# Where the normalized stream, the gated activations and the mixers' outputs begin in SBUF, relative to the weights' tiles

## The chip, the cores and the metric

The kernel runs on one core of a Trainium2 chip. The metric is the device time of one execution in microseconds (us); before the change its median over three runs is 674.23 us (674.15 to 675.28).

## The reference

A decoder trunk of two layers over a stream of 256 positions by 1024 channels, all in float32. Each layer: an RMS norm, one input projection to 2964 columns, four groups of sequence mixers (sparse attention, differential attention, an mLSTM, dilated attention) of 256 columns each, an output projection back into the stream, a second norm and a SwiGLU block of 2816 channels. A last norm follows.

```
for layer in range(DEPTH):
    h = rmsnorm(x, norm_mix[layer])
    z = h @ w_in[layer]                       # 256x1024 @ 1024x2964
    ... four mixers on z's columns ...
    x = x + concat(o_a, o_b, o_c, o_d) @ w_out[layer]          # 1024x1024
    h = rmsnorm(x, norm_ffn[layer])
    x = x + (silu(h @ w_gate[layer]) * (h @ w_up[layer])) @ w_down[layer]
return rmsnorm(x, norm_final)
```

## The kernel before

**Split products.** Every weight arrives by DMA as float32 in a tile of 128x1024 (`wraw`) and is split: ScalarE rounds it to `whi` (float32r, line 232), VectorE subtracts to get `wlo` (line 233). There are four buffers of each, 4096 bytes per partition apiece. The other side of a product is split in the same way: the normalized stream is `hT` (a high and a low part), the SwiGLU activations are `gT`, the mixers' outputs are `oT`. A product is high x high + high x low + low x high, accumulated in PSUM. A matmul holds one operand in the array, 128 columns of it (the stationary one, loaded by a weight load that the profile shows as PEld), and streams the other through (the moving one).

**Two roles.** The projections use the tiles in two ways:

- The stream's side is stationary and the weights move. This is the input projection (`zp`, function `columns`, lines 237 to 239: three matmuls of 512 columns, or 404 in one chunk), and the last down projection of the second layer (`dn` and `dnl`, function `wide`, also lines 237 to 239: three matmuls of 512 columns for three of its five accumulators, and three of 256 for the other two, `dnl`).
- The weights are stationary and the stream's side moves. This is the output projection (`op`, function `wide_T`, from `oT`), the gate and up projections (`f`, function `columns_T`, from `hT`) and the down projection of the first layer (`dn`, function `wide_T`, from `gT`). Where an accumulator has a whole PSUM bank, high and low part of the stream move as one piece of 512 columns under `whi` (line 246), and the high part alone as 256 columns under `wlo` (line 247): a pair. Where two accumulators share a bank, there are three matmuls of 256 columns (lines 237 to 239): a triple.

**Counts.** Over both layers `f` has 576 pairs and 128 triples, `op` 128 triples. The `dn` of the first layer has 132 pairs and 44 triples. The `dn` of the second layer has 198 matmuls of 512 columns and 132 of 256. `zp` has 480 matmuls of 512 columns and 96 of 404.

**Order.** The mixers are cut into steps that a table (`ORDER`) puts between the units of the input projection. The framework's scheduler then fixes one order per engine when the program is built, and moves the first matmuls of `op` in between the last steps of the mixers. Weights are fetched from SyncE's queue, each as soon as its `wraw` buffer is free.

**Places.** The pools take SBUF one after the other: constants, the small parameters (`par`), the weights (`wp`), the working tiles (`work`, where `hT` comes second and `oT` later), the small statistics and the large tile `big` that holds z, and later `gT`. Each tile's start is rounded up to 32 bytes. Before the change the built program has, per partition and in bytes:

| tile | starts at | role of its operand | its start minus the weights' start, modulo 128 |
|---|---|---|---|
| `whi`, `wlo` | 64352 and 80736, then every 4096 | | |
| `hT` (two tiles of 8192) | 99168, 107360 | stationary in `zp`, moving in `f` | 0 |
| `gT` | 180608 | moving in the first `dn`, stationary in the second | 32 |
| `oT` | 152896, then every 2048 | moving in `op` | 96 |

Blocks of `hT`, `gT` and `oT` lie 1024 bytes apart and the slices of a weight tile 512 bytes, so the last column holds for every matmul of a stage (the second half of the chunk of 404 columns excepted).

Of the kernel before, what the change touches and what calls it, by code (L numbers as in the profile page):

```python
# [10 lines left out]
F32 = mybir.dt.float32  # L11
F32R = mybir.dt.float32r
# [6 lines left out]
P = 128  # L19
SEQ = 256  # L20
D = 1024
NH = 4
HD = 64
KB = D // P
D_IN = 2964
D_FF = 2816
NFB = D_FF // P
DEPTH = 2
EPS = 1e-6
WARM = 11  # L30
MID0 = 2
TAIL = 2
MID1 = 2
# [69 lines left out]
def trunk(ctx, tc, xt, w_in, w_out, w_gu, w_dn, gains, gfin, cmpw, chan, rowp, ident_d, kf, kb, out):  # L103
# [4 lines left out]
    par = ctx.enter_context(tc.tile_pool(name="par", bufs=1))  # L108
    wp = ctx.enter_context(tc.tile_pool(name="wp", bufs=2))
    work = ctx.enter_context(tc.tile_pool(name="work", bufs=1))  # L110
# [3 lines left out]
    def mmbank(name):  # L114
        return ps.tile([P, 512], F32, name=name, tag="mm", bufs=4)

    def aux(name):
        return ps.tile([P, 512], F32, name=name, tag="aux", bufs=3)
# [4 lines left out]
    def acc4(name, n=4):  # L123
        return [(mmbank if i < 4 else aux)(f"{name}{i}") for i in range(n)]
# [7 lines left out]
    gain = const.tile([P, DEPTH, 2, KB], F32, name="gain")  # L132
# [9 lines left out]
    bigp = ctx.enter_context(tc.tile_pool(name="bigp", bufs=1))  # L142
# [23 lines left out]
    wb = aux("warm")  # L166
    for _ in range(WARM):
        T.matmul(wb, wz[:, 0:P], wz, start=True, stop=True)
# [18 lines left out]
    def bcast(ap):  # L187
        return ap.partition_broadcast(P)
# [35 lines left out]
    def weight_unit(src, parts=1):  # L224
        n = src.shape[-1]
        raw = wp.tile([P, 1024], F32, name="wraw", bufs=4)
        hi = wp.tile([P, 1024], F32R, name="whi", bufs=4)
        lo = wp.tile([P, 1024], F32R, name="wlo", bufs=4)
        for i in range(parts):
            c = slice(i * n // parts, (i + 1) * n // parts)  # L230
            nc.sync.dma_start(raw[:, c], src[:, c])
            S.activation(hi[:, c], raw[:, c], AF.Copy)  # L232
            V.tensor_tensor(out=lo[:, c], in0=raw[:, c], in1=hi[:, c].bitcast(F32), op=OP.subtract)  # L233
        return hi, lo
# [6 lines left out]
    def product_T(acc, wh, wl, x2, first, last):  # L241


        xh, xl = x2 if isinstance(x2, tuple) else (x2[:, 0], x2[:, 1])
        if acc.shape[-1] == 2 * SEQ:
            T.matmul(acc, wh, x2.rearrange("p a t -> p (a t)"), start=first, stop=False)  # L246
            T.matmul(acc[:, 0:SEQ], wl, xh, start=False, stop=last)  # L247
        else:
            product(acc, wh, wl, xh, xl, first, last)

    def rstd_of(ms, shape, name, eps=None):
# [12 lines left out]
        G.tensor_tensor(out=r, in0=e, in1=nh, op=OP.pow)  # L264
        return r


    class Norm:
        def __init__(self, g):
            self.g = g  # L270

            hl = [work.tile([P, 4, 2, SEQ], F32R, name="hT", bufs=2) for _ in range(2)]
            self.x2 = [hl[k // 4][:, k % 4] for k in range(KB)]
            self.xT = [(x[:, 0], x[:, 1]) for x in self.x2]

        def blocks(self, p):
# [59 lines left out]
    def heads(ap, n):  # L336
        return ap.rearrange("p (n w) -> p n w", n=n)
# [12 lines left out]
    def mixer_a(l, z, d):  # L350
# [25 lines left out]
        for u in range(2):  # L376
            wh, wl = cur['cmpw'][u]
            for i in range(4):
                p, cs = 4 * u + i, slice(i * 256, (i + 1) * 256)
# [34 lines left out]
                T.matmul(pcs[:, (t * 2 + b) * 30:(t * 2 + b + 1) * 30], q0[:, b, t * P:(t + 1) * P],  # L414
                         kcb.rearrange("p a n -> p (a n)"), start=True, stop=True)
        yield
        gs = work.tile([P, 2, 12], F32, name="gs")
        S.activation(gs, z[:, :, COL['ag']:COL['ag'] + 12], AF.Tanh, scale=0.5)
        V.tensor_scalar(gs, gs, 0.5, 0.5, op0=OP.mult, op1=OP.add)

# [418 lines left out]
    d = None  # L839
    for l in range(DEPTH):  # L840
        if l == 0:
            nrm = Norm(gain[:, 0, 0])
        cur['big'] = bigp.tile([P, 2 * D_IN + NS * 1024], F32, name="zbig", tag="big")
        z = cur['big'][:, 0:2 * D_IN].rearrange("p (t c) -> p t c", t=2)
        oT = [None] * 4
# [41 lines left out]
        def columns(src, w, accs, xT, ahead=None, mid=None, steps=()):  # L887

            units = []
            for u in range(KB // 2):  # L890
                if ahead:
                    ahead(u)
                units.append(weight_unit(src[:, u * 2 * w:(u + 1) * 2 * w], 2 if ahead is first_x and u == 0 else 1))
            for u in range(KB // 2):
                wh, wl = units[u]
                for t in range(2):
                    for k in range(2):
                        kk = 2 * u + k
                        xh, xl = (a[:, t * P:(t + 1) * P] for a in xT[kk])
                        cs = slice(k * w, (k + 1) * w)  # L900
                        product(accs[t], xh, xl, wh[:, cs], wl[:, cs], kk == 0, kk == KB - 1)
                if mid and u == mid[0]:
                    mid[1]()
                if u < len(steps) - 1:
                    emit(steps[u])

        def parts_of(pairs):


            return [(b[0][:, j * SEQ:(j + 1) * SEQ], j == 0, j == 1) if len(b) == 1 else (b[j], True, True)  # L910
                    for b in pairs for j in range(2)]
# [16 lines left out]
        def wide_T(src, x2, nblk, name, norm, full=False):  # L928

            if full:
                banks = [[f(f"{name}{i}{j}") for j, f in enumerate(p)]
                         for i, p in enumerate(((mmbank, mmbank), (aux, pvbank), (mmbank, mmbank), (aux,)))]
            else:
                banks = [[b] for b in acc4(name)]

            accs = parts_of(banks)

            def step(kk, m, w):  # L940
                cs = slice(m * P, (m + 1) * P)
                acc, first, last = accs[m]
                product_T(acc, w[0][:, cs], w[1][:, cs], x2(kk), kk == 0 and first, kk == nblk - 1 and last)

            tail = nblk - TAIL
            for kk in range(tail):
                w = weight_unit(src[:, kk * D:(kk + 1) * D])
                for m in range(KB):
                    step(kk, m, w)
                yield  # L950
            ws = [weight_unit(src[:, kk * D:(kk + 1) * D]) for kk in range(tail, nblk)]
            nrm = norm()

            for p in range(KB // 2):
                for m in (2 * p, 2 * p + 1):
                    for kk in range(tail, nblk):
                        step(kk, m, ws[kk - tail])
                if len(banks[p]) == 1:
                    xx = xr[:, 2 * p:2 * p + 2]
                    V.tensor_tensor(out=xx, in0=heads(banks[p][0], 2), in1=xx, op=OP.add)  # L960
                else:
                    for b, m in zip(banks[p], (2 * p, 2 * p + 1)):
                        for i in range(2):
                            V.tensor_tensor(out=xr[:, m], in0=b[:, i * SEQ:(i + 1) * SEQ], in1=xr[:, m], op=OP.add)
                nrm.blocks(p)
                nrm.squares(p)
            return nrm

        def run(g):

            while True:
                try:
                    next(g)
                except StopIteration as r:
                    return r.value
# [34 lines left out]
        for c, (c0, w) in enumerate(CHUNKS):  # L1010
            zacc.append([mmbank(f"zp{t}")[:, 0:w] for t in range(2)])
            columns(w_in[l, :, 8 * c0:8 * (c0 + w)], w, zacc[c], nrm.xT,
                    None if l else {0: first_x, 1: rest_x, 2: rest_par}.get(c),
                    (MID0, first_z) if l == 0 and c == 1 else (MID1, nrm.factors) if c == 0 and l else None,
                    ORDER[l][c].split('|'))
            if c == 1:
                cur['cmpw'] = [weight_unit(cmpw[l, :, u * 1024:(u + 1) * 1024]) for u in range(2)]
            if l or c:
                to_z(c)
            if c == len(CHUNKS) - 1:  # L1020
                fs['o'] = lambda: wide_T(w_out[l], lambda kk: tuple(a[:, kk % 2] for a in oT[kk // 2]), KB, "op",
                                         lambda: Norm(gain[:, l, 1]))
            emit(ORDER[l][c].split('|')[-1])

        def wide(src, opair, nblk, name, rows):
# [24 lines left out]
        nrm = run(gens['o'] if 'o' in gens else fs['o']())  # L1050


        if l + 1 < DEPTH:
            d = load_positions(l + 1)
            load_params(l + 1, d)
        else:
            gf = work.tile([P, D], F32, name="gfin", tag="hT", bufs=2)
            nc.sync.dma_start(gf, bcast(gfin[0]))
        gT = bigp.tile([P, NFB * 2 * SEQ], F32R, name="gT", tag="big").rearrange("p (k a t) -> p k a t", a=2, k=NFB)

        def taken(b, out=None):

# [80 lines left out]
            blk += nk  # L1143
        gp = lambda kk: gT[:, kk]
        if l + 1 < DEPTH:
            nrm = run(wide_T(w_dn[l], gp, NFB, "dn", lambda: Norm(gain[:, l + 1, 0]), True))
        else:
            wide(w_dn[l], gp, NFB, "dn", nrm.rs)

    for t in range(2):  # L1150
# [3 lines left out]
        for h in range(2):  # L1154
            hs = slice(h * 512, (h + 1) * 512)
            sq = work.tile([P, 2, SEQ], F32, name="sq", bufs=2).rearrange("p a b -> p (a b)")
            n = 2 if t and h else 1
# [130 lines left out]
```

## Time and profile before

| | us |
|---|---|
| median of three runs | 674.23 |
| the profiled execution | 673.65 |
| its span from first to last instruction | 671.7 |
| TensorE busy | 657.1 |
| VectorE busy | 481.1 |
| ScalarE busy | 384.6 |

The times below are those of the one profiled execution, which took 673.65 us: 671.7 us of span and 1.95 us around it. The duration that the trace gives a matmul is no price, since matmuls overlap. What a matmul costs is the distance from its start to the start of the next, where nothing is waited for, and that is how the rows of the timeline are read here.

The stages, by the starts of their matmuls in the timeline: the first input projection and the mixers, with the first matmuls of `op` among the mixers' last, to 135 us, the rest of `op` to 149, `f` to 275, `dn` to 336, and in the second layer projection and mixers to 460, the rest of `op` to 476, `f` to 603, `dn` to 665, and then the last norm.

### The profile page before, as it was taken

To read this page: it belongs to the slowest core of one execution; us is meant where nothing else is said; L and a number is where in the kernel's file an instruction comes from. 1 tells how busy PE (TensorE), PEld (TensorE's weight loads), DVE (VectorE), ACT (ScalarE), POOL (GpSimd) and SP (SyncE) were. 2 spreads that over 40 slices of the span, in tenths; PEclk is the share of its full clock that TensorE was granted. 3 is DMA by queue.
4 is the path that set the end of the run, shared out by engine and by line. 5 is a ranking of instruction groups with operands and counts; after the bars stand their busy time and mean duration, and the time that the engine had idled before them with its cause. 6 is when DMAs were issued, how large, how long until landed. Compare 5 with 4: busy or idle time off the path is not lost.

```text
span 671.7 us, 10554 instructions
## 1 busy us (share of the span) xinstructions
PE 657.1 (98%) x3993; PEld 567.1 (84%) x3993; DVE 481.1 (72%) x811; ACT 384.6 (57%) x689; POOL 51.1 (8%) x67
## 2 busy tenths in 40 slices
PE   8899999999999999999999999999999999999996
PEld 5787778899988888899979778779998888888885
DVE  6689698667777877744587969875867777775443
ACT  7466685555555656533466587754655656564332
POOL 0000031100200110000010001140000000000002
PEclk9999999999999999999999999999999999999999
DMA  7865414246566656666647541243556666676631
GB/s 267 295 192 157 143 30 128 64 126 192 175 198 183 190 165 207 188 191 190 181 128 235 160 123 33 63 157 95 158 187 178 190 179 190 185 211 192 188 121 62
DMA packets 31874, 109.09 MB, mean 162 GB/s; under 512 B 3920, under 2 KB 4560, under 8 KB 31824
## 3 DMA queue, kind: packets, MB, share of 16 engines
q1 hardware_dynamic: 31392, 107.89, 53.0%
q8 instruction: 31, 0.51, 0.3%
q10 hardware_dynamic: 432, 0.54, 0.2%
q14 instruction: 19, 0.16, 0.1%
HBM read 107.37 MB, written 1.05 MB: 161 GB/s over the span
## 4 chain that ended last, share of the span: by engine, by line
PE 92%; DVE 3%; ACT 2%; POOL 1%; issue 1%; DMA 1%; POOLq 0%; DVEq 0%; ACTq 0%
PE f L246 20%; PE f L247 10%; PE zp L238 6%; PE zp L239 6%; PE zp L237 5%; PE dn L246 4%; PE dn L238 3%; PE dn L237 3%; PE dn L239 3%; PE dn L247 2%; PE f L237 2%; PE f L239 2%; PE f L238 2%; PE op L239 2%; PE op L237 2%; PE op L238 2%
## 5 line engine op out<-in xcount | busy, mean ns | idle before, releaser
L233 DVE TENSOR_TENSOR wlo<-wraw,whi 128x1024 fp32r<-128x1024 f32 (+2 forms) x201 | 242.0, 1207 | 116.8 <-ACT whi L232 116.0
L232 ACT ACTIVATE whi<-wraw 128x1024 fp32r<-128x1024 f32 (+2 forms) x201 | 210.1, 1047 | 179.2 <-PE f L246 46.0
L246 PE MATMUL f<-hT,whi 128*128 128x512 f32 x576 | 203.6, 399 | 0.0
L247 PE MATMUL f<-hT,wlo 128*128 128x256 f32 x576 | 161.8, 281 | 0.0
L246 PEld LDWEIGHTS f<-hT,whi 128*128 128x128 f32 x576 | 108.2, 188 | 27.0
L247 PEld LDWEIGHTS f<-hT,wlo 128*128 128x128 f32 x576 | 108.8, 189 | 0.0
L238 PE MATMUL zp<-wlo,hT 128*128 128x512 f32 (+1 forms) x192 | 75.7, 395 | 1.3 <-DVE wlo L233 1.3
L237 PE MATMUL zp<-whi,hT 128*128 128x512 f32 (+1 forms) x192 | 74.1, 393 | 1.8 <-ACT whi L232 1.8
L239 PE MATMUL zp<-whi,hT 128*128 128x512 f32 (+1 forms) x192 | 74.9, 391 | 0.0
L246 PE MATMUL dn<-gT,whi 128*128 128x512 f32 x132 | 46.7, 390 | 0.0
L237 PEld LDWEIGHTS zp<-whi,hT 128*128 128x128 f32 x192 | 36.0, 188 | 8.3 <-ACT whi L232 3.1
L238 PEld LDWEIGHTS zp<-wlo,hT 128*128 128x128 f32 x192 | 36.3, 189 | 7.8 <-DVE wlo L233 2.7
L239 PEld LDWEIGHTS zp<-whi,hT 128*128 128x128 f32 x192 | 36.2, 188 | 5.1
L247 PE MATMUL dn<-gT,wlo 128*128 128x256 f32 x132 | 37.2, 282 | 0.0
L237 PE MATMUL f<-hT,whi 128*128 128x256 f32 x128 | 36.9, 288 | 0.0
L237 PE MATMUL op<-oT,whi 128*128 128x256 f32 x128 | 36.8, 288 | 0.0
L239 PE MATMUL op<-oT,wlo 128*128 128x256 f32 x128 | 36.6, 286 | 0.0
L238 PE MATMUL op<-oT,whi 128*128 128x256 f32 x128 | 36.5, 285 | 0.0
L239 PE MATMUL f<-hT,wlo 128*128 128x256 f32 x128 | 36.2, 283 | 0.0
L238 PE MATMUL f<-hT,whi 128*128 128x256 f32 x128 | 36.2, 283 | 0.0
L246 PEld LDWEIGHTS dn<-gT,whi 128*128 128x128 f32 x132 | 24.8, 188 | 4.4
L238 PE MATMUL dn<-wlo,gT 128*128 128x512 f32 x66 | 26.2, 397 | 0.0
(299 smaller groups left out, 1161.1 us busy)
## 6 DMA issues: line engine op xcount, KB each, us to landing
wraw<-in_w_gu_dram SPq DMA_DIRECT2D x88, 512.0 KB, 4.4
wraw<-in_w_dn_dram SPq DMA_DIRECT2D x44, 512.0 KB, 3.7
wraw<-in_w_in_dram SPq DMA_DIRECT2D x39, 512.0 KB, 4.3
wraw<-in_w_out_dram SPq DMA_DIRECT2D x16, 512.0 KB, 3.5
wraw<-in_w_in_dram SPq DMA_DIRECT2D x8, 404.0 KB, 3.2
wraw<-in_cmpw_dram SPq DMA_DIRECT2D x4, 512.0 KB, 4.7
xr<-in_xt_dram SPq DMA_DIRECT2D x4, 256.0 KB, 5.3
chan<-in_chan_dram SPq DMA_DIRECT2D x2, 261.0 KB, 4.7
```

Of the source, the lines that this page charges most:

```text
L232: S.activation(hi[:, c], raw[:, c], AF.Copy)
L233: V.tensor_tensor(out=lo[:, c], in0=raw[:, c], in1=hi[:, c].bitcast(F32), op=OP.subtract)
L237: T.matmul(acc, xh, wh, start=first, stop=False)
L238: T.matmul(acc, xh, wl, start=False, stop=False)
L239: T.matmul(acc, xl, wh, start=False, stop=last)
L246: T.matmul(acc, wh, x2.rearrange("p a t -> p (a t)"), start=first, stop=False)
L247: T.matmul(acc[:, 0:SEQ], wl, xh, start=False, stop=last)
```

## The change

No instruction is added to a compute engine, removed or put in another place on one. What changes is where tiles begin:

- `hT` is one tile of 16416 bytes instead of two of 8192, from a pool slot with one buffer instead of two. Its operand begins at the tile's start where it is stationary (`zp`) and 8 elements, 32 bytes, behind it where it moves (`f`).
- `gT` has 32 bytes more, and begins 32 bytes behind its tile's start in the first layer (moving), at its start in the second (stationary).
- The small tile `gs` goes from the working pool to the parameters' pool, which lies ahead of the weights, and a tile of 32 bytes (`pad`), which nothing uses, stands behind `hT`.

```
-            hl = [work.tile([P, 4, 2, SEQ], F32R, name="hT", bufs=2) for _ in range(2)]
-            self.x2 = [hl[k // 4][:, k % 4] for k in range(KB)]
+            hl = shifted(work.tile([P, KB * 2 * SEQ + SHIFT], F32R, name="hT", bufs=1), KB, moving)
+            self.x2 = [hl[:, k] for k in range(KB)]
...
+    def shifted(a, n, moving):
+        a = a[:, SHIFT if moving else 0:]
+        return a[:, 0:n * 2 * SEQ].rearrange("p (k a t) -> p k a t", a=2, k=n)
...
-        gs = work.tile([P, 2, 12], F32, name="gs")
+        gs = par.tile([P, 2, 12], F32, name="gs")
...
-            nrm = Norm(gain[:, 0, 0])
+            nrm = Norm(gain[:, 0, 0], False)
+
+            work.tile([P, PAD], F32, name="pad")
...
-                                         lambda: Norm(gain[:, l, 1]))
+                                         lambda: Norm(gain[:, l, 1], True))
...
-            gf = work.tile([P, D], F32, name="gfin", tag="hT", bufs=2)
+            gf = work.tile([P, D], F32, name="gfin", tag="hT", bufs=1)
...
-        gT = bigp.tile([P, NFB * 2 * SEQ], F32R, name="gT", tag="big").rearrange("p (k a t) -> p k a t", a=2, k=NFB)
+        gT = shifted(bigp.tile([P, NFB * 2 * SEQ + SHIFT], F32R, name="gT", tag="big"), NFB, l + 1 < DEPTH)
...
-            nrm = run(wide_T(w_dn[l], gp, NFB, "dn", lambda: Norm(gain[:, l + 1, 0]), True))
+            nrm = run(wide_T(w_dn[l], gp, NFB, "dn", lambda: Norm(gain[:, l + 1, 0], False), True))
```

`SHIFT` and `PAD` are 8. In the built program the weights' tiles then start at 64448 and 80832, `hT` at 99264, `gT` at 180672 and `oT` at 152960, and the differences become:

| stage | moving side | the stream's side minus the weights' start, modulo 128: before | now |
|---|---|---|---|
| `zp` | weights | 0 | 0 |
| `op` | mixers' outputs | 96 | 64 |
| `f` | stream | 0 | 32 |
| `dn`, first layer | gated activations | 32 | 32 |
| `dn`, second layer | weights | 32 | 0 |

The weights' own start modulo 64 goes from 32 to 0.

Since `hT` has one buffer now, the last norm's gain (`gfin`, which takes that slot at the very end) can be fetched only when all of `hT` has been read, and not half of it. On SyncE's queue near the end of the second layer's `f`, before the change, where `w_dn` is the down projection's weight:

```order
36 L231 DMA wraw<-in_w_dn_dram 128x1024 x5
37 L1058 DMA gfin<-in_gfin_dram 128x1024
38 L231 DMA wraw<-in_w_dn_dram 128x1024 x17
```

and with the change:

```order
36 L233 DMA wraw<-in_w_dn_dram 128x1024 x7
37 L1068 DMA gfin<-in_gfin_dram 128x1024
38 L233 DMA wraw<-in_w_dn_dram 128x1024 x15
```

The fetch of `gfin` has moved behind two weights. On the other engines the same instructions stand in the same order, with the same waits, but for the number of the DMA's semaphore near this place.

## Rows read from the trace of the kernel before

**Rows 1.** The page: busy time of TensorE and VectorE with share of the span and instructions; the granted clock in 40 slices of the span; the chain that ended last, by engine.

```profile
PE 657.1 (98%) x3993; PEld 567.1 (84%) x3993; DVE 481.1 (72%) x811; ACT 384.6 (57%) x689; POOL 51.1 (8%) x67
...
PEclk9999999999999999999999999999999999999999
...
PE 92%; DVE 3%; ACT 2%; POOL 1%; issue 1%; DMA 1%; POOLq 0%; DVEq 0%; ACTq 0%
```

**Rows 2.** Waits of TensorE over the whole span: who waited for whom, us in total, times, the longest.

```profile
PE zp L237 <- ACT whi L232: 1.8, 2, 1.1
PE cT L357 <- ACT zbig L987: 1.7, 2, 1.4
PE zp L238 <- DVE wlo L233: 1.3, 3, 0.5
```

**Rows 3.** Busy time of each engine by stage: the stretch in us and its length, then busy us (instructions) of PE, PEld, DVE, ACT and POOL, the granted clock, the DMA engines' busy share and GB/s.

```profile
143.00:160.00 17.00, 17.00 (x145) 17.00 (x144) 14.72 (x23) 11.42 (x18) 0.00 (x0) 1.00 0.52 151
...
173.00:275.00 102.00, 102.00 (x581) 88.44 (x580) 79.12 (x107) 59.16 (x89) 15.56 (x10) 1.00 0.63 186
275.00:336.00 61.00, 61.00 (x397) 55.80 (x396) 32.43 (x40) 25.81 (x30) 0.00 (x0) 1.00 0.66 193
336.00:460.00 124.00, 121.62 (x717) 100.00 (x716) 100.46 (x215) 82.17 (x188) 16.24 (x20) 1.00 0.40 122
...
501.00:603.00 102.00, 102.00 (x580) 88.44 (x579) 77.14 (x105) 59.51 (x89) 0.00 (x0) 1.00 0.64 187
603.00:665.00 62.00, 62.00 (x332) 52.78 (x330) 30.37 (x34) 25.09 (x32) 3.14 (x3) 1.00 0.50 152
```

**Rows 4.** Timeline of TensorE, starts and modelled durations in us: the first pair of `f` and the first matmul of `dn` behind the last one, in the first layer and in the second. Between the two starts lie 288 pairs each time.

```profile
173.23 0.40 PE L246 MATMUL f<-hT,whi 128*128 128x512 f32 x1
...
274.99 0.40 PE L246 MATMUL dn<-gT,whi 128*128 128x512 f32 x1
...
501.28 0.40 PE L246 MATMUL f<-hT,whi 128*128 128x512 f32 x1
...
603.05 0.40 PE L237 MATMUL dn<-whi,gT 128*128 128x512 f32 x1
```

**Rows 5.** The same view, the end of the first layer's `dn`: twelve matmuls of 256 columns, four triples, from the first of these rows to the last, which is the next layer's first.

```profile
334.76 0.28 PE L237 MATMUL dn<-gT,whi 128*128 128x256 f32 x1
334.87 0.28 PE L238 MATMUL dn<-gT,whi 128*128 128x256 f32 x1
...
336.04 0.28 PE L239 MATMUL dn<-gT,wlo 128*128 128x256 f32 x1
336.16 0.39 PE L237 MATMUL zp<-whi,hT 128*128 128x512 f32 x1
```

**Rows 6.** The same view, the last triples of `f` ahead of its first pair: the first of the seven matmuls of 256 columns that lie between it and the pair at 173.23, and the last.

```profile
172.39 0.28 PE L239 MATMUL f<-hT,wlo 128*128 128x256 f32 x1
...
173.11 0.28 PE L239 MATMUL f<-hT,wlo 128*128 128x256 f32 x1
```

**Rows 7.** The same view, two undisturbed stretches of `zp` of 512 columns, one in each layer: from the first row to the second twelve matmuls, and from the third to the fourth twelve.

```profile
34.09 0.39 PE L237 MATMUL zp<-whi,hT 128*128 128x512 f32 x1
...
36.80 0.39 PE L237 MATMUL zp<-whi,hT 128*128 128x512 f32 x1
...
365.90 0.40 PE L237 MATMUL zp<-whi,hT 128*128 128x512 f32 x1
...
368.66 0.39 PE L237 MATMUL zp<-whi,hT 128*128 128x512 f32 x1
```

**Rows 8.** The same view, the second layer's `dn`: nine matmuls of 512 columns lie between its start at 603.05 and the first row here, and six of 256 between the two rows here.

```profile
605.15 0.28 PE L237 MATMUL dnl<-whi,gT 128*128 128x256 f32 x1
...
605.87 0.40 PE L237 MATMUL dn<-whi,gT 128*128 128x512 f32 x1
```

**Rows 9.** The same view, `op`: eighteen matmuls of 256 columns from the first row to the second.

```profile
136.21 0.28 PE L237 MATMUL op<-oT,whi 128*128 128x256 f32 x1
...
138.34 0.28 PE L237 MATMUL op<-oT,whi 128*128 128x256 f32 x1
```

**Rows 10.** The instructions of line 246, which are the 512 columns of a pair: durations in ns, least, median and most, and first and last start.

```profile
L246 PE MATMUL f<-hT,whi x576: 395/398/403, 173.2 to 602.7; 128*128 128x512 f32 x192
...
L246 PE MATMUL dn<-gT,whi x132: 390/390/399, 275.0 to 334.4; 128*128 128x512 f32 x132
```

**Rows 11.** What ScalarE waited for between 180 and 260 us, in `f`: us in total, times, the longest.

```profile
ACT whi L232 <- PE f L246: 14.1, 12, 1.8
```

**Rows 12.** Timeline of SyncE's queue around the fetch of the last norm's gain; and of the view of that tile its first readers, on GpSimd (ns, first and last start in us), and the fetch's time from issue to landing.

```profile
585.68 11.98 SPq L231 DMA_DIRECT2D wraw<-in_w_dn_dram  x5
597.72 1.21 SPq L1058 DMA_DIRECT2D gfin<-in_gfin_dram  x1
599.87 11.73 SPq L231 DMA_DIRECT2D wraw<-in_w_dn_dram  x5
...
L1163 POOL TENSOR_TENSOR y<-xs,gfin x2: 1290/1296/1302, 657.9 to 663.5; 128x512 f32<-128x512 f32 x2
...
DMA to landing us min/median/max: 6.8/6.8/6.8
```

More of the change, by code (lines that the diff above doesn't have):

```diff
@@ L30 @@
 WARM = 11
+SHIFT = 8
+PAD = 8
 MID0 = 2
@@ L265, in rstd_of, with __init__ @@
         return r
+    def shifted(a, n, moving):
+        a = a[:, SHIFT if moving else 0:]
+        return a[:, 0:n * 2 * SEQ].rearrange("p (k a t) -> p k a t", a=2, k=n)
     class Norm:
-        def __init__(self, g):
+        def __init__(self, g, moving):
             self.g = g
-            hl = [work.tile([P, 4, 2, SEQ], F32R, name="hT", bufs=2) for _ in range(2)]
-            self.x2 = [hl[k // 4][:, k % 4] for k in range(KB)]
+            hl = shifted(work.tile([P, KB * 2 * SEQ + SHIFT], F32R, name="hT", bufs=1), KB, moving)
+            self.x2 = [hl[:, k] for k in range(KB)]
             self.xT = [(x[:, 0], x[:, 1]) for x in self.x2]
```

## The prediction

> **What bounds the kernel now.** I read the page first: TensorE is busy for 657.1 of 671.7 us, 92% of the chain that ended last are its instructions, and its clock is granted in full, at the upper of its two levels (2.4 GHz), in every slice and stage [rows 1, 3]. Its waits come next: the three longest lines come to 4.8 us over the whole span, all in the input projection and the mixers, none in `op`, `f` or `dn` [rows 2]. The table by stage says the same: in `f`, in `dn` and in the pure part of `op` TensorE is busy without a gap, while VectorE and ScalarE have room (79.12 and 59.16 us of 102 in `f`) [rows 3]. So in these stages time is the number of matmuls times the distance from one start to the next. The matmuls' counts, sizes, order and waits stay as they are, so the change can work only through that distance, and the question is whether the distance depends on where the two operands lie.
>
> It does differ between stages that do the same work. A pair, 512 columns under `whi` and then 256 under `wlo`, takes (274.99 - 173.23) / 288 = 353.3 ns in the first layer's `f`, and (603.05 - 501.28) / 288 = 353.4 ns in the second's [rows 4]. The first layer's `dn` is made of the same pairs and of triples. Four triples at its end take 336.16 - 334.76 = 1.40 us, 116.7 ns a matmul [rows 5]. From 274.99 [rows 4] to 336.16 [rows 5] are 61.17 us; less 132 matmuls at 116.7 ns, 15.40 us, 45.77 us are left for 132 pairs: 346.7 ns. The triples of `f` go the same way: (173.23 - 172.39) / 7 = 120.0 ns a matmul [rows 4, 6] against 116.7 in `dn`. What the two stages don't share is the distance of the moving operand from the weights, modulo 128 bytes: 0 in `f`, 32 in `dn`. The durations carry the same mark: the 512 columns show 395 to 403 ns in `f`, and 390 both at the least and at the median in `dn` [rows 10].
>
> Where the weights move, the sign is the other way. `zp` has distance 0 and takes (36.80 - 34.09) / 12 = 225.8 ns per 512 columns in one clean stretch and (368.66 - 365.90) / 12 = 230.0 in another [rows 7]. The second layer's `dn` has distance 32 and takes (605.15 - 603.05) / 9 = 233.3 [rows 4, 8]. I have no mechanism for this turn of sign, so I carry a price over only between stages in which the same side moves.
>
> **The change part by part.** Each number is a count times a difference of the distances above.
>
> - `f`, pairs: distance 0 becomes 32, which is that of the first `dn`, with the same side moving and the same order of matmuls. 576 pairs x (353.3 - 346.7) = 3.8 us off. Bounds: 0, if the place has no part in it, and 3.8, since `f` has the dearest pairs of the trace and `dn` the cheapest.
> - `f`, triples: 384 matmuls x (120.0 - 116.7) = 1.3 us off, with bounds 0 and 1.3 for the same reason.
> - The second `dn`, 512 columns: distance 32 becomes 0, that of `zp`. `zp` gives 225.8 to 230.0; I take their middle, 228, and 233.3 for the row replaced: 198 x 5.3 = 1.0 us off, bounds 0.7 (by 230.0) and 1.5 (by 225.8). Its 132 matmuls of 256 columns now take (605.87 - 605.15) / 6 = 120.0 ns [rows 8]. No row has this size at distance 0 with the weights moving; by the triples' two distances it could gain 0.4 us or, since 120.0 is already the worse of the two, nothing. I take 0.
> - `op`: distance 96 becomes 64, which no stage has. It takes (138.34 - 136.21) / 18 = 118.3 ns now [rows 9], between the 116.7 and the 120.0 of the other triples. Bounds for 384 matmuls: 0.6 us off, if 64 is like 32, 0.65 us more, if it is like 0. I take 0, in the middle of two ends that are equally near.
> - The first `dn` and `zp` keep their distances (32 and 0): 0, and a cost only if something other than the distance counts (a rival below).
> - The mixers' own matmuls see their tiles move by 64 to 160 bytes against each other. Of the 3993 matmuls [rows 1] 3222 belong to the projections, 771 don't; a tenth of these at the 3.3 ns of a triple's matmul would be 0.25 us either way. I take 0.
> - One buffer for `hT` instead of two tiles: the next norm writes into it only after `dn` has begun, long after `f` has read it, so no wait arises. The one instruction that moves is the fetch of the last gain. It was issued at 597.72, between two groups of weights, and will be issued when `f` ends, near 603, ahead of an eighth weight that can't go earlier: its `wraw` buffer is freed by a split that itself waits for `f`'s last unit. The fetch lands after 6.8 us [rows 12], and the gain is first read at 657.9. 0; if the weight behind it were held up, a delay of one issue, 1.2 us [rows 12], is covered by the three split units ahead.
>
> Does the gain reach the end? In `f` TensorE is followed by everybody: ScalarE's split waited 14.1 us for it within 80 us [rows 11], so weights, at 186 GB/s and 0.63 of the DMA engines' time, are ahead [rows 3]. With pairs 1.9% shorter VectorE's load goes from 78% to 79%. Nothing else comes due.
>
> The sum for the profiled execution: 3.8 + 1.3 + 1.0 = 6.1 us off 673.65, which is 671.7 of span and 1.95 around it: 667.55. The profiled execution lies 0.58 us below the median of the runs shown, so the median should go from 674.23 to 668.1.
>
> A rule speaks against all of this. TensorE has one SBUF read port for the moving operand and another for the weight load, independent of each other (the Trainium skill, "TensorE: Matmul & The Clock Gate", Part 2), and its own ports never wait for anyone ("SBUF — State Buffer", section on the two separate sides). By that rule a shift of 32 bytes, which is also a whole number of that page's 16-byte lines, is worth nothing, and the time stays at 674.2; the rows by which I decide between the two are those of `f` and the first `dn`, and they are 6.6 ns a pair apart without the rule having a reason for it.
>
> **The rivals.**
>
> 1. Places have no part in it, and `f` is slower than `dn` because of its company: there VectorE is busy for 78% of the time (79.12 of 102) and evicts PSUM, in `dn` for 53% (32.43 of 61) [rows 3]. Then nothing changes: 674.2. For it: the stages do differ in that. Against it: the second `dn` has the least company, VectorE 30.37 of 62 us, and is slower than `zp`, which runs where VectorE is at 81% (100.46 of 124) [rows 3]; and the two `f` stages agree to 0.1 ns a pair though GpSimd works for 15.56 us in one and not at all in the other [rows 3, 4]. This is also what the ports' rule of the page on TensorE would make of the change.
> 2. The place of each operand counts, and not the distance: in `f` and `zp` both sides begin at 32 modulo 64, in the first `dn` the stream's side begins at 0, in the second the stationary side does. A moving stream is then cheap at 0, and a stationary operand dear at 0. Now `f`'s stream stays at 32 and gains nothing. The first `dn`'s moves from 0 to 32 and takes `f`'s prices: 132 x 6.6 + 132 x 3.3 = 1.3 us more. `zp`'s stationary side goes from 32 to 0 and takes the second `dn`'s price: 480 x 5.3 = 2.5 us more. Together 3.8 us more, 678.0: slower. It decides as soon as the distance by itself is worth under half of the 6.1. For it: it explains the turn of sign. Against it: by it `op` and the triples of the first `dn` (both moving at 0, weights at 32) should cost the same, and they are 118.3 and 116.7 [rows 5, 9]; and a fixed cost of a place should be the same in each matmul, while `f`'s 512 columns spread over 395 to 403 ns and `dn`'s hardly do [rows 10], as two streams would that meet now and then.
> 3. Half of the gain is eaten: `f` runs into VectorE or the weights, or `op` and the mixers lose by their new distances. 671.2. Against it the room named above.
>
> **How the numbers follow.** A measurement of this kernel can tell about 0.2%, 1.35 us, from no change. The forecast, 668.1, has a chance of 0.80; its own range, from the bounds of `op`, the second `dn`, the mixers and a part of the pairs that might not settle, is 666 to 670.3. Rival 3 has 0.06, rival 1 0.09, rival 2 0.05. Faster is the forecast and rival 3, 0.86; same is rival 1, 0.09; slower is rival 2, 0.05. The range that leaves out no more than 2 in 10 goes from 665.8 to 671.5: outside it are rivals 1 and 2 and a few in a hundred of the forecast's own tails.
>
> **What will show it.** Right: 288 pairs of `f` in 99.9 us instead of 101.8 in both layers, their 512 columns shown with one duration and not three, triples of `f` 117 ns apart, the first `dn` still 61.2 us long, the second near 60.8 from 61.9, and `zp`'s clean stretches at 226 to 230 ns. `op` will show what a distance of 64 is worth. Wrong: pairs of `f` at 353 with `dn` as it was (rival 1), or the first `dn` at 353 a pair and `zp` above 233 (rival 2). If `f`'s pairs shrink and its end does not come earlier, TensorE will show waits in `f` that it does not have now.

## The result and the profile after

The changed kernel takes 668.25 us, the median of four runs (667.16 to 669.01), beside 674.19 us for the kernel before, measured with it (673.55 to 675.28). The ratio is 0.9909, with a 95% interval of 0.9888 to 0.993. The forecast was 668.1. The profiled execution took 667.16 us with a span of 665.3, 6.4 us less than the 671.7 before.

The page of the changed kernel: busy time by engine, the granted clock in 40 slices, and the chain that ended last, by engine [rows 1].

```profile
PE 650.3 (98%) x3993; PEld 565.8 (85%) x3993; DVE 480.3 (72%) x811; ACT 384.6 (58%) x689; POOL 51.3 (8%) x67
...
PEclk9999999999999999999999999999999999999998
...
PE 91%; DVE 3%; ACT 2%; issue 1%; POOL 1%; DMA 1%; POOLq 0%; DVEq 0%; ACTq 0%
```

The same 3993 matmuls at the same granted clock (but for a little in the last slice) keep TensorE busy for 6.8 us less; the other engines' busy time hardly moves. The chain is still TensorE's. So nothing was taken out of the path; its steps became shorter. Where, the timeline of TensorE says (starts and modelled durations in us; line 248 is line 246 of before, and 239 to 241 are 237 to 239). It answers to [rows 4 to 9].

```profile
34.18 0.39 PE L239 MATMUL zp<-whi,hT 128*128 128x512 f32 x1
...
36.90 0.39 PE L239 MATMUL zp<-whi,hT 128*128 128x512 f32 x1
...
136.21 0.28 PE L239 MATMUL op<-oT,whi 128*128 128x256 f32 x1
...
138.25 0.28 PE L239 MATMUL op<-oT,whi 128*128 128x256 f32 x1
...
171.03 0.28 PE L239 MATMUL f<-hT,whi 128*128 128x256 f32 x1
...
172.08 0.39 PE L248 MATMUL f<-hT,whi 128*128 128x512 f32 x1
...
271.92 0.39 PE L248 MATMUL dn<-gT,whi 128*128 128x512 f32 x1
...
333.08 0.39 PE L239 MATMUL zp<-whi,hT 128*128 128x512 f32 x1
...
461.90 0.28 PE L239 MATMUL op<-oT,whi 128*128 128x256 f32 x1
...
464.02 0.28 PE L239 MATMUL op<-oT,whi 128*128 128x256 f32 x1
...
497.55 0.39 PE L248 MATMUL f<-hT,whi 128*128 128x512 f32 x1
...
597.39 0.39 PE L239 MATMUL dn<-whi,gT 128*128 128x512 f32 x1
...
599.45 0.28 PE L239 MATMUL dnl<-whi,gT 128*128 128x256 f32 x1
...
658.54 0.28 PE L241 MATMUL dnl<-whi,gT 128*128 128x256 f32 x1
```

How to read it: between 172.08 and 271.92 lie the first layer's 288 pairs of `f`, 99.84 us or 346.7 ns each, and between 497.55 and 597.39 the second layer's, 99.84 again. Before it was 101.76 and 101.77 [rows 4]. The first `dn` takes 333.08 - 271.92 = 61.16 us (61.17 before). In the second, nine matmuls of 512 columns take 599.45 - 597.39 = 2.06 us, 228.9 ns each, against 233.3 [rows 4, 8]. Starts are shown to 10 ns, so a price that is read from nine or twelve matmuls is good to about 1 ns only. Eighteen matmuls of `op` take 2.04 us (113.3 ns) in the first layer and 2.12 us (117.8 ns) in the second, against 118.3 [rows 9]. Nine triple matmuls of `f` take 1.05 us, 116.7 ns each, against 120.0 [rows 6]. The clean stretch of `zp`, twelve matmuls from 34.18 to 36.90, gives 226.7 ns.

The durations of line 248 (ns, least, median and most) have become one number where `f` had three [rows 10]:

```profile
L248 PE MATMUL f<-hT,whi x576: 390/390/392, 172.1 to 597.0; 128*128 128x512 f32 x192
...
L248 PE MATMUL dn<-gT,whi x132: 390/390/390, 271.9 to 331.3; 128*128 128x512 f32 x132
```

The first layer's `f`, with the columns of [rows 3]:

```profile
172.00:271.00 99.00, 99.00 (x574) 87.79 (x573) 77.88 (x105) 58.45 (x86) 15.73 (x10) 1.00 0.64 191
```

TensorE is busy without a gap, VectorE for 77.88 of 99 us: the others followed the shorter pairs. Waits tell the same, first TensorE's over the span [rows 2], then ScalarE's between 180 and 260 us [rows 11] (us in total, times, the longest):

```profile
PE zp L239 <- ACT whi L234: 2.1, 2, 1.1
PE cT L365 <- ACT zbig L997: 1.7, 2, 1.4
PE zp L240 <- DVE wlo L235: 1.3, 3, 0.5
```

```profile
ACT whi L234 <- PE f L248: 16.1, 15, 1.7
```

No wait of TensorE in `f` has come up, and the split still waits for TensorE. The fetch of the last norm's gain now goes out right behind the end of `f`, at 597.58 us on SyncE's queue [rows 12], and nothing waits for it:

```profile
583.23 14.19 SPq L233 DMA_DIRECT2D wraw<-in_w_dn_dram  x6
597.58 0.33 SPq L1068 DMA_DIRECT2D gfin<-in_gfin_dram  x1
```

The 6.4 us of span by place: the pairs of `f` give 1.92 + 1.93 = 3.85; the triples, whose mean over both layers goes from 119.8 to 116.7 ns, 384 x 3.1 = 1.2; the second `dn`, from its start to the start of its last matmul, goes from 61.86 to 658.54 - 597.39 = 61.15, so 0.71. What is left, 0.64, is `op`'s. The part of it that stands behind the mixers, 249 of its 384 matmuls, takes 13.59 us instead of 14.16 in the first layer and 15.39 instead of 15.47 in the second. Projection and mixers take what they took: 135.20 us for 135.18, and 124.03 in the second layer both times. By the starts of its consecutive matmuls the mean of `op` was 118.3 and 118.4 ns before, and is now 113.8 (166 of them) and 117.4 (172).

One stretch shows a price almost without company. In the second `dn`, behind the last split of a weight, no DMA moves anything and VectorE is busy for a third of the time, before and now (columns as in [rows 3]):

```profile
656.60:662.20 5.60, 5.60 (x26) 4.52 (x25) 1.91 (x4) 1.69 (x5) 1.85 (x2) 1.00 0.00 0
...
650.30:655.80 5.50, 5.50 (x26) 4.51 (x25) 1.83 (x4) 1.61 (x5) 1.84 (x2) 1.00 0.00 0
```

In each lie 24 matmuls of 512 columns, from the first of these rows to the second before, and from the third to the fourth now:

```profile
656.60 0.40 PE L239 MATMUL dn<-whi,gT 128*128 128x512 f32 x1
...
662.19 0.28 PE L237 MATMUL dnl<-whi,gT 128*128 128x256 f32 x1
...
650.33 0.40 PE L241 MATMUL dn<-whi,gT 128*128 128x512 f32 x1
...
655.79 0.28 PE L239 MATMUL dnl<-whi,gT 128*128 128x256 f32 x1
```

They took 5.59 us at a distance of 32, 232.9 ns each, and take 5.46 at 0, 227.5 each. The other engines do the same in both, and no weight arrives or is split, so the difference of 5.4 ns is not theirs.

### The profile page after: what moved, and what is told of

The parts are those of the page before. It is cut to its first block, busy times and chain, and to the rows that moved or that the text cites. A ratio compares the mean times of both kernels' runs of the same rounds, so it can differ in the third digit from the quotient of the medians.

```text
span 665.3 us, 10554 instructions
## 1 busy us (share of the span) xinstructions
PE 650.3 (98%) x3993; PEld 565.8 (85%) x3993; DVE 480.3 (72%) x811; ACT 384.6 (58%) x689; POOL 51.3 (8%) x67
## 3 DMA queue, kind: packets, MB, share of 16 engines
HBM read 107.37 MB, written 1.05 MB: 163 GB/s over the span
## 4 chain that ended last, share of the span: by engine, by line
PE 91%; DVE 3%; ACT 2%; issue 1%; POOL 1%; DMA 1%; POOLq 0%; ACTq 0%; DVEq 0%
PE f L248 20%; PE f L249 10%; PE zp L240 6%; PE zp L241 6%; PE zp L239 5%; PE dn L248 4%; PE dn L240 3%; PE dn L239 3%; PE dn L241 3%; PE dn L249 2%; PE f L239 2%; PE f L241 2%; PE f L240 2%; PE op L239 2%; PE op L240 2%; PE op L241 2%
## 5 line engine op out<-in xcount | busy, mean ns | idle before, releaser
L248 PE MATMUL f<-hT,whi 128*128 128x512 f32 x576 | 199.8, 390 | 0.0
```

## The experiments

The theory: what counts is the distance from the weights' tiles to the stream's tiles, modulo 128 bytes. Its rivals: the company of the other engines, for which the last stretch above has spoken; the place of each operand by itself; a shape of the law (a signed difference, a period, a meeting with the next weight load). Except for the first kernel and the last, all have the tiles of the changed kernel with free offsets for `hT` in `zp` and `f` and for `gT`, per layer and in elements of 4 bytes, and differ in these numbers. In each run a price is read as above, as the time from the first pair to the first matmul of `dn`, over 288. Line numbers lie a little further on in some of these kernels: line 248 can be 251 or 253.

### All tiles moved, no distance changed

The kernel before, with 32 bytes ahead of the weights:

```
+    par.tile([P, 8], F32, name="ppad")
```

> The kernel before, with 32 unused bytes ahead of the weights: weights, stream, activations and mixers' outputs all begin 32 bytes later, so every place modulo 64 changes and every distance stays. If the distance sets the price, nothing changes: 674.2 within 0.2%, f's pairs at 353, the first dn's at 347, zp at 226 to 230, the second dn at 233 to 234 per 512 columns. If each operand's own place sets it (the second rival), f's stream now begins at 0 modulo 64 and its pairs fall to 347 (3.8 us), the first dn's rise to 353, zp's change too.

Measured: 673.94 us (673.81 to 675.74), ratio 0.9998 (0.9989 to 1.0008). The timeline of TensorE:

```profile
173.40 0.40 PE L248 MATMUL f<-hT,whi 128*128 128x512 f32 x1
...
275.15 0.40 PE L248 MATMUL dn<-gT,whi 128*128 128x512 f32 x1
...
501.47 0.40 PE L248 MATMUL f<-hT,whi 128*128 128x512 f32 x1
...
603.24 0.40 PE L239 MATMUL dn<-whi,gT 128*128 128x512 f32 x1
```

101.75 and 101.77 us for 288 pairs are 353.3 and 353.4 ns, as before. Every place modulo 64 is another one, every distance is kept, and every price is kept. Rival 2 of the prediction, the own place of each operand, falls.

### The two parts of the change apart

`f` alone at 32, all else as before, and all else as in the change with `f` at 0 (offsets of `zp`, `f` and `gT` by layer):

```
+PAD = 24; ZP = (0, 0); FF = (8, 8); GG = (0, 0)     # f alone
+PAD = 16; ZP = (0, 0); FF = (0, 0); GG = (8, 0)     # all but f
```

> Only f's distance is changed (0 to 32); op (96), the first dn (32), zp (0) and the second dn (32) stay at the distances of the kernel before. If each stage pays by its own distance: 3.9 us off by the pairs and 1.2 by the triples, 5.1 in all, 0.9924 of the kernel before; op at 118.3 and the second dn at 233.7 ns as before.

Measured: 668.84 us (668.36 to 670.2), ratio 0.9918 (0.9905 to 0.9931). The first layer's `f`:

```profile
173.26 0.39 PE L251 MATMUL f<-hT,whi 128*128 128x512 f32 x1
...
273.11 0.39 PE L251 MATMUL dn<-gT,whi 128*128 128x512 f32 x1
```

Pairs of `f` cost 346.7 ns in both layers, `op` 118.3 and 118.4, the second `dn`'s 512 columns 232.8.

> The changed kernel with f left at distance 0: op at 64, the second dn at 0. By the stages of the changed kernel: second dn 0.8 us off, op 0.75 off, 1.5 in all, 0.998 of the kernel before; f's pairs at 353.

Measured: 673.72 us (672.14 to 674.51), ratio 0.9983 (0.9972 to 0.9993). Pairs of `f` at 353.3 ns, the second `dn` at 229.5, `op` at 117.6 and 117.3. The two parts add up: 0.82% and 0.17% off make 0.99%, and the whole change has 0.91% (0.70 to 1.12). Most of the gain, 0.82 of 0.99, is `f`'s.

This run also shows what a total can hide. Its profiled execution has a span of 672.5 us, more than the 671.7 before, though `f` costs the same and `dn` and `op` less. The table by stretches (columns as in [rows 3]) says why:

```profile
30.00:32.00 2.00, 0.81 (x3) 0.38 (x3) 1.23 (x1) 2.00 (x4) 0.00 (x0) 1.00 0.92 319
32.00:33.00 1.00, 1.00 (x4) 0.87 (x5) 0.93 (x1) 0.29 (x3) 0.00 (x0) 0.88 0.78 266
33.00:34.00 1.00, 1.00 (x4) 0.71 (x4) 0.97 (x6) 0.10 (x1) 0.00 (x0) 0.50 0.90 279
```

For some 3.5 us in the first `zp` the granted clock is at the lower of its two levels, behind 2 us in which TensorE was busy for 0.81, and the timeline has a matmul of 512 columns start every 0.43 us there:

```profile
32.72 0.59 PE L243 MATMUL zp<-wlo,hT 128*128 128x512 f32 x1
33.11 0.63 PE L244 MATMUL zp<-whi,hT 128*128 128x512 f32 x1
33.53 0.63 PE L243 MATMUL zp<-wlo,hT 128*128 128x512 f32 x1
...
36.36 0.40 PE L244 MATMUL zp<-whi,hT 128*128 128x512 f32 x1
```

From the first to the last of these rows nine matmuls take 3.64 us; at 227 ns they would take 2.04, so the stretch costs 1.6 us. In the changed kernel's trace TensorE was busy for 0.96 of the same 2 us, and the clock stayed up. The profiled executions of four other kernels here have this stretch too, and two more have one near 8 us. This is why each price here is read inside its stage.

### Other distances

Four kernels with distances that no stage had:

```
+FF = (16, 24); ZP = (0, 8);  GG = (0, 24)      # f at 64 and 96
+FF = (4, 32);  ZP = (0, 24); GG = (16, 16)     # f at 16 and 128
+FF = (6, 10);  ZP = (0, 4);  GG = (12, 28)     # f at 24 and 40
+FF = (40, 20); ZP = (0, 28); GG = (40, 4)      # f at 160 and 80
```

> The changed kernel with other distances (stream's side minus weights, modulo 128): f 64 in the first layer and 96 in the second, first dn 0, zp of the second layer 32, second dn 96. If the price goes by the distance of the moving side minus the stationary one (so that 32 with the stream stationary is the same as 96 with the stream moving): the first dn's pairs rise to 353 and its triples to 120; f's triples take 113 to 118 in the first layer and 118 in the second, as op did at 64 and 96; zp of the second layer rises to 233; the second dn, which is then at 32 in that reading, falls to 228 or under. If the sign really turns with the side that moves, the second dn stays at 230 to 234. If places alone count, f at 64 and 96 costs what 0 and 32 cost.

Measured (one time, 674.14 us), the first layer's `dn` from its start to the next layer's first matmul:

```profile
275.21 0.39 PE L251 MATMUL dn<-gT,whi 128*128 128x512 f32 x1
...
337.63 0.40 PE L242 MATMUL zp<-whi,hT 128*128 128x512 f32 x1
```

At 0 it takes 62.42 us, at 32 it took 61.17: its pairs cost 353.2 ns and its triples 119.7, the prices of `f` at 0. `zp` at 32 costs 233.0. Both were as forecast. `f` costs 348.9 ns a pair at 64 and 350.0 at 96, and not what 0 and 32 cost. Its triples cost 117.8 at 64, where 113 to 118 was expected, and 119.8 at 96, where `op`'s 118 was expected: `op`'s price did not carry over. The second `dn` at 96 gave 233.3 (nine matmuls from 603.40 to 605.50), not 228 or less: the reading by a signed difference falls.

> The changed kernel with other distances: f 16 in the first layer and 128 in the second, first dn 64, zp of the second layer 96, second dn 64. If the distance counts modulo 128, f of the second layer is back at 353 a pair and 120 a triple's matmul although it begins 128 bytes behind the place of the kernel before; 16 lies between 0 and 32: 347 to 353. zp of the second layer is at 32 in the reading moving minus stationary: 226 to 228 and steadier than before. The first dn at 64 has triples at 113 to 118. If places modulo 64 count, f of the second layer costs what 0 and 64 do.

Measured (one time, 675.5 us), the timeline of `f` in the first layer:

```profile
172.54 0.40 PE L251 MATMUL f<-hT,whi 128*128 128x512 f32 x1
...
276.22 0.40 PE L251 MATMUL dn<-gT,whi 128*128 128x512 f32 x1
```

103.68 us, 360.0 ns a pair: the dearest of all, where 347 to 353 was expected. At 128 `f` takes 351.1, near 0 but not its equal. The first `dn` at 64 takes 353.3 a pair and 117.8 a triple's matmul. `zp` at 96 gave 234.2 (368.34 to 371.15, twelve matmuls), where 226 to 228 was expected. 16 and `zp` were misses.

> The changed kernel with finer distances: f 24 in the first layer and 40 in the second, first dn 48, zp of the second layer 16, second dn 112. So far a pair costs 353 at 0, 360 at 16, 347 at 32, 349 to 353 at 64, 350 at 96. If the price is a smooth function of the distance with its least near 32: 24 between 347 and 360, 40 and 48 between 347 and 351. If only whole steps of 32 bytes count: 24 as 0 (353), 40 and 48 as 32 (347), zp at 16 as at 0 (229) and the second dn at 112 as at 96 (234).

Measured (one time, 673.85 us): `f` at 24 353.3, at 40 346.7; the first `dn` at 48 349.6; `zp` at 16 232.0, the second `dn` at 112 233.8. The pairs are what the smooth function gives: 24 lies midway between 360.0 at 16 and 346.7 at 32, and 40 and 48 between 347 and 351. That only whole steps of 32 bytes count falls by 48, and by `zp` at 16, where 229 was expected.

> The changed kernel with f at 160 in the first layer and 80 in the second, first dn at 160, zp of the second layer at 112, second dn at 16. If the distance counts modulo 128, 160 is like 32: pairs of f and of the first dn at 346.6, triples at 116.7. 80 lies between 64 (348.9) and 96 (350.0). The second dn at 16 and zp at 112 cost about what 112 and 16 did: 232 to 234 per 512 columns, all dearer than at 0.

Measured (one time, 672.82 us): `f` at 160 346.7, the same as at 32, the first `dn` at 160 347.2; `f` at 80 353.3 (500.44 to 602.19), where 348.9 to 350.0 was expected; `zp` at 112 233.0, the second `dn` at 16 233.1. So 128 more is the same for 32, and nearly so for 0, and a guess by the neighbours missed again: with 80 dearer than both 64 and 96, the price is no smooth function with one least either.

| distance, modulo 128 unless above it | ns a pair (512 and 256 columns), weights stationary | ns per 512 columns, weights moving |
|---|---|---|
| 0 | 353.2 to 353.4 | 226.7 to 230.0 |
| 16 | 360.0 | 232.0 to 233.1 |
| 24 | 353.3 | |
| 32 | 346.7 | 232.8 to 233.7 |
| 40 | 346.7 | |
| 48 | 349.6 (`dn`) | |
| 64 | 348.9 (`f`), 353.3 (`dn`) | 232.7 |
| 80 | 353.3 | |
| 96 | 350.0 | 233.3 to 234.2 |
| 112 | | 233.0 to 233.8 |
| 128 | 351.1 | |
| 160 | 346.7 (`f`), 347.2 (`dn`) | |

What follows: with nothing but 512 columns, 0 is cheap and every other distance that was tried costs 3 to 7 ns more in the same stage. The pair has a pattern of its own, with its best at 32 and 40, and at 64 `f` and `dn` differ by 4.4 ns at one distance, so the distance isn't the whole of it. A mean can hide a rhythm, too: consecutive pairs of `f` take 349, 350 and 361 ns by turns at 0, but 353 or 354 each at 24, where the mean is the same, and 360 each at 16.

### Is it the side that moves, or the form?

The prediction had no mechanism for the turn of sign. This kernel gives `f` in both layers and the first `dn` matmuls of 512 columns only, with the weights still stationary; `f` is at 0 in the first layer and at 32 in the second:

```
-            T.matmul(acc[:, 0:SEQ], wl, xh, start=False, stop=last)
+            T.matmul(acc, wl, x2.rearrange("p a t -> p (a t)"), start=False, stop=last)
```

> The changed kernel with the pairs made of two matmuls of 512 columns (the low part of the stream is multiplied by wlo too, which adds a term to the product): f at 0 in the first layer, at 32 in the second, first dn at 32. It is some 60 us longer. The stream still moves. If the turn of sign comes with the side that moves, a matmul of 512 columns costs 236 at 0 and 228 at 32. If it comes with the form (nothing but 512 columns, as in zp and the second dn), it costs 229 at 0 and 234 at 32.

Measured (one time, 748.79 us; the wider matmuls are work added), the first and the last rows of `f` in each layer, 576 matmuls apart:

```profile
173.22 0.40 PE L251 MATMUL f<-hT,whi 128*128 128x512 f32 x1
...
303.80 0.40 PE L251 MATMUL dn<-gT,whi 128*128 128x512 f32 x1
...
544.70 0.39 PE L251 MATMUL f<-hT,whi 128*128 128x512 f32 x1
...
679.09 0.40 PE L242 MATMUL dn<-whi,gT 128*128 128x512 f32 x1
```

130.58 us is 226.7 ns a matmul at 0, and 134.39 us is 233.3 at 32: the prices of `zp` and of the second `dn`, with the other side moving. The first `dn` at 32 gives 233.3 too. The turn of sign comes with the form of the matmuls in a row, all of 512 columns or 512 and 256 by turns, and not with the side that moves. Pairs with the weights moving were not run.

### Which of two meetings counts?

Weight loads run beside the matmuls (PEld is busy for 87.79 of 99 us in `f`). To see whether its price goes by its own weights or by the next, `wlo`'s tiles go 32 bytes off `whi`'s. First with pairs, then with 512 columns only:

```
         hi = wp.tile([P, 1024], F32R, name="whi", bufs=4)
+        if 'wpad' not in cur:
+            cur['wpad'] = wp.tile([P, 8], F32, name="wpad", bufs=1)
         lo = wp.tile([P, 1024], F32R, name="wlo", bufs=4)
```

> The changed kernel with 32 unused bytes between the whi and the wlo tiles, so that a stream has two distances. f's first layer: 32 from whi, 0 from wlo; second layer: 64 from whi, 32 from wlo. While the 512 columns stream under whi, the weights that are loaded are wlo's. If the price comes from the stream meeting the next weight load, the 512 columns of the first layer cost what distance 0 costs (236 on average, spread over 232 to 241) and the second layer's 228. If it comes from the operand that is already in place (whi), the first layer's 512 columns cost 228 and the second layer's what 64 costs.

Measured (one time, 671.27 us), with `whi` at a distance of 32 and `wlo` at 0 in the first layer:

```profile
174.97 0.39 PE L253 MATMUL f<-hT,whi 128*128 128x512 f32 x1
...
274.17 0.39 PE L253 MATMUL dn<-gT,whi 128*128 128x512 f32 x1
```

99.20 us, 344.4 ns a pair, the least of all runs: 226.4 ns for the 512 columns and 118.1 for the 256. The expected 236 for the 512 columns, which now run beside the load of a tile at 0, did not come. In the second layer, with 64 and 32, it was 231.5 and 117.4, 348.9 together, which is what 64 costs with both tiles at 64. So `whi`'s distance sets most of a pair, but not all: with `wlo` at 32 as well a pair took 346.7, and the first `dn`, with `whi` at 32 and `wlo` at 0 like `f`, takes 346.3 here and not 344.4. As a kernel it gains nothing over the change: `zp`'s 512 columns rise to 233, since one of its two tiles is no longer at 0.

> As both_512 (two matmuls of 512 columns instead of a pair; the low part of the stream is multiplied by wlo too), with wlo's tiles 32 bytes off whi's: f's first layer at 32 from whi and 0 from wlo, its second at 64 from whi and 32 from wlo. With one distance for both, 512 columns cost 226.7 at 0 and 233.3 at 32. While the columns stream under whi the weights of the next matmul, wlo's, are loaded, and the other way round. If a stream pays by its distance from the load that goes on meanwhile, the first layer's matmuls under whi cost 227 and those under wlo 233. If it pays by the weights that it streams under, those under wlo cost 227 and those under whi 233.

Measured (one time, 753.25 us), consecutive rows of `f` in the first layer, `whi` at 32 and `wlo` at 0:

```profile
198.82 0.39 PE L253 MATMUL f<-hT,whi 128*128 128x512 f32 x1
199.05 0.40 PE L254 MATMUL f<-hT,wlo 128*128 128x512 f32 x1
...
202.56 0.39 PE L253 MATMUL f<-hT,whi 128*128 128x512 f32 x1
```

Sixteen matmuls in 3.74 us, 234 ns; over the stage 231.7 under `whi` and 235.0 under `wlo`. Neither 227 and 233 nor 233 and 227, the two forecasts: with one tile off 0 the two cost 233.3 on the mean, as much as with both at 32. With 64 and 32 in the second layer it was 230.8 and 232.5. Which meeting it is stays open.

### The changed kernel again

> The changed kernel unaltered, once more: 0.991 of the kernel before. In its first profile op cost 113.8 ns a matmul in the first layer and 117.4 in the second at one and the same distance (64). If the program fixes which of the two a stage falls into, it does so again; if it is chance in each execution, the two layers may show 114 or 117 in any combination.

Measured, in five runs: 667.62 us (666.48 to 668.78), ratio 0.9908 (0.9895 to 0.9922). The second layer's `op`, where the first profile had 117.8 ns:

```profile
461.32 0.28 PE L239 MATMUL op<-oT,whi 128*128 128x256 f32 x1
...
463.37 0.28 PE L239 MATMUL op<-oT,whi 128*128 128x256 f32 x1
```

Eighteen matmuls in 2.05 us, 113.9 ns; the stage has 114.2 on the mean, where the first profile had 117.4. The same program with the same places has two prices in one stage, from one execution to the other. All kernels with `op` at 64 from both weight tiles show one or the other as the mean of a layer: 113.8 to 114.7 or 117.3 to 117.6, both below the 118.3 to 118.4 of the kernels with `op` at 96. What chooses between them stays open.

## Why the prediction was right, and where it was not

**The bound, and the price by starts.** Right. Time in `f`, `dn` and `op` was a count of matmuls times the distance of their starts, and shortening it shortened the span by as much; no wait came in its place.

**`f`, pairs (3.8 us).** 3.85 us, and 346.7 ns in both layers, to the tenth. The step that carried it was taking the price from the first `dn`, which had the same form of matmuls in the same order. That it was the distance is shown by three runs: all tiles moved together changes nothing, `f` alone brings 0.82%, and the first `dn` put at 0 takes `f`'s old 353. One sign that the prediction named is none, though: the 512 columns shown with one duration and not three. At 16, the dearest distance, all 288 in the first layer's `f` show 398 ns.

**`f`, triples (1.3 us).** 1.2: the 120.0 was read from seven matmuls, and the mean over the stage is 119.8.

**The second `dn` (1.0 us, bounds 0.7 and 1.5).** 0.71, at the lower bound. Its 512 columns went from 233.7 to 229.4 ns on the mean (longer gaps left out), where the middle of two stretches of `zp`, 228, was taken. Its 256 columns rose from 118.2 to 118.8, which takes back 0.08; the 120.0 that the prediction gave them was read from six. One gap of 282 ns at the last split takes back 0.05 more. The clean stretch of `zp` gives 226.7; the second `dn`, three accumulators of 512 columns and then two of 256, does not reach it on the mean. The bound of 1.5 rested on 225.8, which is 226.7 by the trace's starts in whole ns.

**`op` (0, bounds 0.6 off and 0.65 more).** The one term that left its bounds: 0.64 us off in the first profile and 1.2 in the second, although only 249 of the 384 matmuls stand on the path. The step that failed is to bound 64 by the prices of the triples at 32 and at 0. 113.8 ns lies below both, so the bound of 116.7 was none. And no one price was there to be forecast: the same program gave 117.4 and 114.2 in the second layer.

**The turn of sign, left without a mechanism.** Carrying prices only between stages in which the same side moves was safe, but for the wrong reason. With nothing but 512 columns, stationary weights follow `zp`'s prices (226.7 at 0, 233.3 at 32). What must be the same is the sequence of column counts.

**The first `dn`, `zp`, the mixers and the gain's fetch (0).** 61.16 us for 61.17; 226.7 ns in `zp`; the projection and the mixers as long as before to 0.02 us; no wait behind the fetch.

**The rivals.** Rival 1, no part for places, falls by `f` itself: its company is the same (VectorE busy for 78% before, 79% now), its price is not, and by the stretch of the second `dn` in which no DMA runs. Nor does the time of 674.2 that goes with the Trainium skill's rule hold, by which the ports for the moving operand and for the weight load are independent ("TensorE: Matmul & The Clock Gate", Part 2): the trace disagrees with its use here by 6.6 ns a pair between 32 and 0, and by 13.3 between 32 and 16. Rival 2 falls by the kernel whose tiles were all moved (0.9998), and fell by the change itself: the first `dn`'s stream went from 0 to 32 modulo 64 and kept its 61.16 us. But the argument against it from the spread of the durations was no argument, since distances alone give both a spread (at 0) and none (at 16). Rival 3, half of the gain eaten, did not come about, for the reason given: `f` had room.

**The total.** The triples and the second `dn` were 0.1 and 0.3 us too large, `op` 0.6 too small; in the span that leaves 6.4 for 6.1. That the median came within 0.15 us of the forecast is in part that cancelling, and luck besides: the four runs lie between 667.16 and 669.01.

## What to carry to other kernels

Where TensorE is busy without a gap, compare the distance of matmul starts between stages of the same form. If it differs, look at where the tiles of the two operands begin relative to each other; here offsets and paddings of 32 bytes were together worth 0.9% of the whole, and added no instruction. Don't carry a price to another distance or another sequence of column counts by analogy, and don't read it from the total: measure each distance in its stage, as the guesses for 16, 80, `zp` at 96 and `op`'s 64 missed.

## What was not expected of the hardware

The distance matters in steps finer than the 32 bytes to which tiles are rounded: pairs cost 353.3, 360.0, 353.3, 346.7 and 346.7 ns at 0, 16, 24, 32 and 40 bytes. That moving read and weight load hinder each other in SBUF would fit that only relative places count, but no run here shows the mechanism; where exactly a collision lies, its period (0 and 128 differ by 2.2 ns) and why `f` and `dn` part at 64 are open.

One program has two prices in the second layer's `op`, 117.4 and 114.2 ns on the mean, between executions with full clock. And no stage's mean for 512 columns came below 226.4 ns here (under `whi` with `wlo` apart), with a weight load for each matmul. The Trainium skill gives an isolated matmul's gap as columns over 2.4 plus 2.5 ns ("TensorE: Matmul & The Clock Gate", "Back-to-back issue gap"), about 216 for 512; no run here comes as low.
